# A hybrid scan and attention backbone on one core: the scan's decays in three wide operations, and the rotary tables made behind the scan

## The chip, the cores and the metric

The kernel runs on one core of a Trainium2 chip. The metric is the device time of one execution in microseconds, median of several runs. The core has TensorE (matmuls into PSUM), VectorE, ScalarE and GpSimd (elementwise work), and SyncE, whose queue SP issues every DMA of this kernel. Each engine works through a list of its own in order; semaphores join the lists. In the profile they are PE (PEld for its weight loads), DVE, ACT, POOL and SP.

## The reference

Two layers over 1024 latent and 256 context tokens, model width 1024. Each layer normalises and modulates its input, multiplies it by one input projection, and feeds three groups of heads: a bidirectional state space scan (8 heads of 64, 2 groups, state 128, chunks of 128 tokens), grouped-query attention and differential attention. Their outputs go through one output projection, a norm, a gate and the residual. The part that the change touches, cut:

```python
def ssd_scan(x, dt, a, bm, cm, init_state):
    xd = f(x * dt[..., None])
    a_cum = jnp.cumsum(f(dt * a), axis=2)
    lmat = segsum_exp(jnp.moveaxis(a_cum, -1, 2))
    y_diag = jnp.einsum('bcqhn,bcshn,bchqs,bcshp->bcqhp', cc, bc, lmat, xd)
    ...
    y_off = jnp.einsum('bcqhn,bchpn,bcqh->bcqhp', cc, states_in, jnp.exp(a_cum))
    return y_diag + y_off, final_state

def segsum_exp(cs):
    diff = cs[..., :, None] - cs[..., None, :]
    return jnp.exp(jnp.where(tril, diff, -jnp.inf))
```

So for each chunk and head there is a 128x128 matrix of decays exp(a_q - a_s) in each direction, weighted by the step size dt of the source token. And the queries and keys of the grouped-query heads are normalised and rotated by cosine and sine tables that depend on the position.

## The kernel before

All 10 token tiles (0 and 1 context, 2 to 9 latent) are kept as columns of 128 tokens. Per layer the work goes in stages:

- The transposed part of the input projection (x, B, C), a convolution over five taps and a SiLU (`conv_tile`). Beside it ScalarE and GpSimd split the output projection's weights (tile wos, `split_wout`), whose loads wof come over SP.
- The token-row part of the projection in five column chunks (`tok_chunk`): z, differential q and k, grouped q, k and v, differential v, gates. A chunk's weights are loaded (wf) and split into leading and trailing halves (wh, wl); then for each token tile 24 matmuls run into a bank prj, of which there are two. The bank goes off by ScalarE and VectorE: for z a tanh (th) on ScalarE and a product on VectorE; for q and k a copy raw (three buffers), rotation (`rope`), a split st, a transpose on TensorE (qps), a copy tt and stores.
- Beside the chunks z, differential q and k, and differential v runs the scan (`scan`), a generator that the loop over token tiles advances. Per chunk c it loads xb (x and B in token rows), ab (the running sums of both directions on all 128 partitions, 8 heads of 128 columns each, 1 MB, one buffer) and bct. D and W are the two halves of ab. VectorE subtracts each head's own sum (L775) and takes the minimum with the other direction's (L776), ScalarE takes the exponential of all of D (L778). Then for each head ScalarE multiplies the masked product gf of C and B by the forward step size into W (L781), VectorE adds the backward one (L782), and GpSimd multiplies W by D (L784). TensorE's 8 products of W with x (pd, L792) follow, and `y_off` (po, yt) and `state_step` (xs, stp, Sf, Sb) bring in the states. The next load of ab needs those products done.
- The chunk of grouped q, k and v runs when the scan is over, with the final norm of the scan's output (`finish`: yf, zt) between its token tiles. Its rotation needs the tables C and S (cosine and sine with the gains folded in), which before are made ahead of the scan: two loads (cosg, sing), four products on GpSimd (L933), four on VectorE (L934).
- The gates' chunk, then attention and the output projection.

The instructions are not in the order of the code: a scheduler, run when the program is built, goes by priorities and its own estimates of durations, and lays down one fixed list per engine. Pools are released tile by tile, and a later tile in the same memory waits for the readers of the earlier one. The lines that matter:

```python
D, W = ab[:, 0], ab[:, 1]
for h in range(8):
    V.tensor_scalar(D[:, h], D[:, h], acs[:, 0, c, h:h + 1], None, op0=ALU.subtract)
    V.scalar_tensor_tensor(D[:, h], W[:, h], acs[:, 1, c, h:h + 1], D[:, h],
                           op0=ALU.subtract, op1=ALU.min)
S_.activation(D, D, AF.Exp)
```

## Time and profile before

| what | value |
|---|---|
| time, median of 3 runs | 2101.39 us (2097.04 to 2106.61) |
| span of the profiled execution | 2095.2 us |
| TensorE busy | 1822.2 us (87%) |
| VectorE busy | 1565.1 us (75%) |
| ScalarE busy | 1041.9 us (50%) |
| GpSimd busy | 1162.7 us (55%) |
| mean granted TensorE clock | 0.935 |

The span is that of one profiled execution, from its first to its last instruction; the median is 6.2 us longer, and the runs lie from 1.8 to 11.4 us above the span. Busy time counts what an engine executes, and an operation that is held up while it runs counts as busy for all of it. The granted clock is the share of full speed that TensorE was given.

### The profile page before, as it was taken

To read this page: it belongs to the slowest core of one execution; us is meant where nothing else is said; L and a number is where in the kernel's file an instruction comes from. 1 tells how busy PE (TensorE), PEld (TensorE's weight loads), DVE (VectorE), ACT (ScalarE), POOL (GpSimd) and SP (SyncE) were. 2 spreads that over 40 slices of the span, in tenths; PEclk is the share of its full clock that TensorE was granted. 3 is DMA by queue.
4 is the path that set the end of the run, shared out by engine and by line. 5 is a ranking of instruction groups with operands and counts; after the bars stand their busy time and mean duration, and the time that the engine had idled before them with its cause. 6 is when DMAs were issued, how large, how long until landed. Compare 5 with 4: busy or idle time off the path is not lost.

```text
span 2095.2 us, 31014 instructions
## 1 busy us (share of the span) xinstructions
PE 1822.2 (87%) x9936; PEld 1475.8 (70%) x9936; DVE 1565.1 (75%) x4103; ACT 1041.9 (50%) x1955; POOL 1162.7 (55%) x1007
## 2 busy tenths in 40 slices
PE   5899999898979999888988797998798898989885
PEld 4587777777767668777765486877777776768773
DVE  5777567777759878799858477577687787888974
ACT  4444233334347766676634354233333676767651
POOL 4535355654227657668735335556543577877741
PEclk9899999899989999999989898998998999999997
DMA  9157557856795988586665148668656956457455
GB/s 289 44 197 235 174 178 205 265 176 203 213 267 167 283 257 261 165 248 201 216 218 186 33 151 283 207 188 247 218 157 208 278 172 180 140 157 212 145 183 184
DMA packets 360003, 418.61 MB, mean 200 GB/s; under 512 B 38752, under 2 KB 252832, under 8 KB 359840
## 3 DMA queue, kind: packets, MB, share of 16 engines
q1 hardware_dynamic: 359840, 416.64, 64.0%
q8 instruction: 78, 1.28, 0.2%
q14 instruction: 85, 0.70, 0.1%
HBM read 282.18 MB, written 134.38 MB: 199 GB/s over the span
## 4 chain that ended last, share of the span: by engine, by line
PE 38%; DVE 26%; DMA 16%; POOL 6%; issue 6%; ACT 4%; SPq 3%; DVEq 0%; POOLq 0%; ACTq 0%
DVE pt L1244 6%; PE sc L1242 4%; DMA ab<-acs 3%; PE tp L1373 3%; PE prj L962 3%; PE prj L961 3%; PE prj L963 3%; PE ops L343 2%; PE ops L344 2%; PE ops L345 2%; PE po L1416 2%; PE po L1415 2%; DMA op<-o 2%; DMA q<-dq 2%; DMA wof<-in_wout_dram 2%
## 5 line engine op out<-in xcount | busy, mean ns | idle before, releaser
L129 POOL TENSOR_TENSOR pl<-pf,ph 128x512 fp32r<-128x512 f32 x283 | 374.2, 1327 | 197.2 <-DVE ph L1395 80.4
L1244 DVE TENSOR_SCALAR_CACHE_REDUCE pt<-sc 128x512 f32<-128x512 f32 (+1 forms) x600 | 335.3, 587 | 71.6 <-PE sc L1242 62.8
L1257 ACT ACTIVATE pt<-pt,nm 128x1280 f32<-128x1280 f32 x192 | 262.4, 1366 | 132.1 <-DVE nm L1255 130.1
L961 PE MATMUL prj<-wh,u 128*128 128x512 f32 (+1 forms) x768 | 298.8, 391 | 27.1 <-DVE th L967 13.7
L962 PE MATMUL prj<-wl,u 128*128 128x512 f32 (+1 forms) x768 | 295.9, 386 | 8.0 <-POOL wl L129 5.3
L963 PE MATMUL prj<-wh,u 128*128 128x512 f32 (+1 forms) x768 | 293.9, 384 | 0.0
L1373 PE MATMUL tp<-ident,pt 128*128 128x128 f32 x1312 | 209.5, 283 | 4.9 <-ACT pf L1383 3.5
L1416 PE MATMUL po<-pl,vt 128*128 128x256 f32 x644 | 184.4, 308 | 18.6 <-POOL pl L129 14.9
L1415 PE MATMUL po<-ph,vt 128*128 128x256 f32 x644 | 187.7, 304 | 14.5 <-ACT ot L1420 6.3
L1383 ACT COPY pf<-tp 128x512 f32<-128x512 f32 x289 | 166.6, 580 | 66.3 <-PE tp L1373 30.9
L961 PEld LDWEIGHTS prj<-wh,u 128*128 128x128 f32 x768 | 153.1, 200 | 54.3 <-DVE th L967 15.6
L1373 PEld LDWEIGHTS tp<-ident,pt 128*128 128x128 f32 x1312 | 160.4, 145 | 29.5 <-ACT pf L1383 8.2
L962 PEld LDWEIGHTS prj<-wl,u 128*128 128x128 f32 x768 | 153.6, 200 | 33.5 <-POOL wl L129 6.6
L1242 PE MATMUL sc<-dk,q 128*128 128x512 f32 (+1 forms) x400 | 148.2, 416 | 31.2 <-DVE pt L1244 21.3
L963 PEld LDWEIGHTS prj<-wh,u 128*128 128x128 f32 x768 | 153.6, 200 | 23.2
L1416 PEld LDWEIGHTS po<-pl,vt 128*128 128x128 f32 x644 | 126.8, 197 | 39.4 <-POOL pl L129 27.4
L1415 PEld LDWEIGHTS po<-ph,vt 128*128 128x128 f32 x644 | 127.1, 197 | 29.5 <-ACT ot L1420 9.5
L607 DVE SCALAR_TENSOR_TENSOR cacc<-craw,hw,cacc 128x1284 f32<-128x1284 f32 (+1 forms) x64 | 118.5, 1853 | 33.4 <-ACT cacc L604 21.9
L582 PE MATMUL prj<-u,wTh 128*128 128x512 f32 x256 | 108.4, 423 | 23.4 <-DVE u L210 17.0
L343 PE MATMUL ops<-y,wo 128*128 128x512 f32 (+1 forms) x304 | 119.0, 391 | 7.4 <-DMA y<-y 6.8
L1296 POOL TENSOR_SCALAR pt<-pt,cc 128x256 f32<-128x256 f32 x64 | 103.1, 1612 | 38.1 <-DVE cc L1288 16.1
L1242 PE MATMUL sc<-gk,q 128*128 128x256 f32 (+1 forms) x400 | 111.7, 384 | 14.1 <-DVE pt L1244 11.8
(287 smaller groups left out, 4448.1 us busy)
## 6 DMA issues: line engine op xcount, KB each, us to landing
wo<-wo SPq DMA_DIRECT2D x80, 512.0 KB, 4.8
wm<-in_wmod_dram SPq DMA_DIRECT2D x48, 512.0 KB, 5.9
dk<-dk SPq DMA_DIRECT2D x16, 1280.0 KB, 7.9
ab<-acs SPq DMA_DIRECT2D x18, 1024.0 KB, 7.6
wo<-wos SPq DMA_DIRECT2D x32, 512.0 KB, 3.6
wf<-in_wtok_dram SPq DMA_DIRECT2D x64, 256.0 KB, 4.0
y<-y SPq DMA_DIRECT2D x30, 512.0 KB, 5.5
op<-o SPq DMA_DIRECT2D x48, 256.0 KB, 4.4
```

What stands on the lines that cost most here:

```text
L129: eng.tensor_tensor(out_, full, hi.bitcast(F32), op=ALU.subtract)
L343: TE.matmul(o, wa[:, k], y[:, :, 0], start=first, stop=False)
L961: TE.matmul(ps[:, c0:], uh, wh[k][:, c0:], start=k == 0, stop=False)
L962: TE.matmul(ps[:, c0:], uh, wl[k][:, c0:], start=False, stop=False)
L963: TE.matmul(ps[:, c0:], ul, wh[k][:, c0:], start=False, stop=k == KT - 1)
L1242: TE.matmul(ps[:, 0:b - a].rearrange("p (t c) -> p t c", c=P), q[:, jb.q0 + j], kt[:, a // P:b // P], start=x == 0, stop=x == len(qq) - 1)
L1244: V.tensor_scalar(ts[r][:, a:b], ps[:, 0:b - a], -1.0, None, op0=ALU.mult, op1=ALU.min, accum_out=mts[r][:, i:i + 1])
L1257: S_.activation(e, e, AF.Exp, bias=nm, scale=-1.0, accum_out=jb.s2[:, j, mp_:mp_ + 1])
L1373: TE.transpose(tp[:, j * P:(j + 1) * P], jb.pt[2 * hf + j % 2][:, cs(2 * s + j // 2)], ident)
L1383: S_.copy(pf[:, :w_], tp[:, :w_])
L1415: TE.matmul(o, vv, a[:, c], start=k == 0, stop=False)
L1416: TE.matmul(o, vv, b[:, c], start=False, stop=k == jb.nk - 1)
```

## The change

In the scan, GpSimd subtracts the sums of all heads from D in one operation of 128x1024, VectorE does it for W in one, and takes the minimum in one. The products with the forward step sizes go into a new tile rw (one buffer), those with the backward ones into W, all sixteen on ScalarE, and VectorE adds the two tiles in one operation. The rotary tables are made by a function `tables` that is called when the scan is over, in a pool `rot2` of its own that takes memory which the scan has left. Comments and docstrings are gone in the new file too, and below the scan its line numbers are 4 to 8 higher.

```diff
+        def over_q(tab_, dr, c):
+            return tab_[:, dr, c, :].unsqueeze(2).to_broadcast([P, 8, P])
...
                     D, W = ab[:, 0], ab[:, 1]
+                    G.tensor_tensor(D, D, over_q(acs, 0, c), op=ALU.subtract)
+                    V.tensor_tensor(W, W, over_q(acs, 1, c), op=ALU.subtract)
+                    V.tensor_tensor(D, W, D, op=ALU.min)
+                    S_.activation(D, D, AF.Exp)
+                    R = sp.tile([P, 8, P], F32, name="rw", tag="rw")
                     for h in range(8):
-                        V.tensor_scalar(D[:, h], D[:, h], acs[:, 0, c, h:h + 1], None, op0=ALU.subtract)
-                        V.scalar_tensor_tensor(D[:, h], W[:, h], acs[:, 1, c, h:h + 1], D[:, h],
-                                               op0=ALU.subtract, op1=ALU.min)
-                    S_.activation(D, D, AF.Exp)
+                        S_.activation(R[:, h], gf[:, 0, h // 4], AF.Copy, scale=dts[:, 0, c, h:h + 1])
                     yield
                     for h in range(8):
-                        S_.activation(W[:, h], gf[:, 0, h // 4], AF.Copy, scale=dts[:, 0, c, h:h + 1])
-                        V.scalar_tensor_tensor(W[:, h], gf[:, 1, h // 4], dts[:, 1, c, h:h + 1], W[:, h],
-                                               op0=ALU.mult, op1=ALU.add)
+                        S_.activation(W[:, h], gf[:, 1, h // 4], AF.Copy, scale=dts[:, 1, c, h:h + 1])
+                    V.tensor_tensor(W, W, R, op=ALU.add)
                     G.tensor_tensor(W, W, D, op=ALU.mult)
...
         with pool("rot") as rp, pool("tokc", 2) as ck:
-            cosg = ck.tile([P, 8, 32], F32, name="cosg", tag="st", bufs=2)
-            sing = ck.tile([P, 8, 32], F32, name="sing", tag="st", bufs=2)
-            SY.dma_start(cosg, ropeg[0])
-            SY.dma_start(sing, ropeg[1])
...
+            def tables(rp):
+                cosg = rp.tile([P, 8, 32], F32, name="cosg")
+                sing = rp.tile([P, 8, 32], F32, name="sing")
+                SY.dma_start(cosg, ropeg[0])
+                SY.dma_start(sing, ropeg[1])
...
-            with pool("trp2", 4, space=PSUM) as trp_, pool("fin", 2) as fp, pool("wsplit2", 2) as wo_:
+            with pool("trp2", 4, space=PSUM) as trp_, pool("fin", 2) as fp, pool("wsplit2", 2) as wo_, \
+                    pool("rot2") as rp2:
+                tables(rp2)
                 for t, _ in enumerate(tok_chunk(ck, 2, 0)):
```

The body of `tables` is the code that stood in the place of the dots: the gains gn, then the four products each.

What the scheduler makes of it, at three places. First VectorE's list at one chunk of the scan in layer 0; before:

```order
L721 TENSOR_TENSOR Sf<-stp,Sf 128x512
L775 TENSOR_SCALAR ab<-ab,acs 128x128 x6
L776 SCALAR_TENSOR_TENSOR ab<-ab,acs 128x128
L775 TENSOR_SCALAR ab<-ab,acs 128x128
...
L776 SCALAR_TENSOR_TENSOR ab<-ab,acs 128x128 x5
L782 SCALAR_TENSOR_TENSOR ab<-gf,dts,ab 128x128
L776 SCALAR_TENSOR_TENSOR ab<-ab,acs 128x128
L782 SCALAR_TENSOR_TENSOR ab<-gf,dts,ab 128x128 x4
L967 SCALAR_TENSOR_TENSOR th<-th,prj 128x512
```

and now, with GpSimd's list at a chunk some steps later behind it:

```order
L725 TENSOR_TENSOR Sf<-stp,Sf 128x512
L779 TENSOR_TENSOR ab<-ab,acs 128x1024
L973 SCALAR_TENSOR_TENSOR th<-th,prj 128x512
L780 TENSOR_TENSOR ab<-ab 128x1024
L788 TENSOR_TENSOR ab<-ab,rw 128x1024
```

```order
L778 TENSOR_TENSOR ab<-ab,acs 128x1024
L713 TENSOR_TENSOR xs<-xbb,coef 128x512
L895 TENSOR_TENSOR raw<-raw,t_2876 128x512
L723 TENSOR_TENSOR Sf<-Sf,etot 128x512
L129 TENSOR_TENSOR st<-raw,st 128x8x32
L789 TENSOR_TENSOR ab<-ab 128x1024
L723 TENSOR_TENSOR Sb<-Sb,etot 128x512
L895 TENSOR_TENSOR raw<-raw,t_2958 128x512
```

On VectorE the product th that frees a projection bank stands between the two wide operations, where it stood behind a row of small ones. On GpSimd the subtraction L778 stands ahead of the state inputs xs, a rotation sum raw and a split st; before, no operation of its list needed ab until L784.

Second, ScalarE's list where layer 1 passes from the convolution to the scan; before:

```order
L679 CAST wos<-wof 128x512
L625 COPY xt<-xtp 128x256
L625 COPY xt<-xtp 128x512 x2
L679 CAST wos<-wof 128x512 x2
L966 ACTIVATE th<-prj 128x512 x2
L679 CAST wos<-wof 128x512
L966 ACTIVATE th<-prj 128x512 x2
L778 ACTIVATE ab<-ab 128x1024
```

and now:

```order
L679 CAST wos<-wof 128x512
L972 ACTIVATE th<-prj 128x512 x2
L625 COPY xt<-xtp 128x256
L625 COPY xt<-xtp 128x512 x2
L679 CAST wos<-wof 128x512 x2
L972 ACTIVATE th<-prj 128x512
L679 CAST wos<-wof 128x512
L972 ACTIVATE th<-prj 128x512 x3
L781 ACTIVATE ab<-ab 128x1024
```

Two tanh moved ahead of the copies xt and two casts. In the scan's later chunks of the new list the eight products rw stand ahead of the exponential.

Third, VectorE's list behind the scan in layer 1, now:

```order
L907 TENSOR_TENSOR raw<-raw,nrr 128x384
L931 TENSOR_SCALAR gnqg<-pk_11893 128x64
L931 TENSOR_SCALAR gnkg<-pk_11893 128x64
L910 TENSOR_TENSOR raw<-raw,gnkg 128x128 x2
L940 SCALAR_TENSOR_TENSOR Skg<-sing,gnkg 128x8x32 x2
L940 SCALAR_TENSOR_TENSOR Sqg<-sing,gnqg 128x8x32 x2
L886 TENSOR_TENSOR t_15544<-raw,Sqg 128x4x32
```

The products with the sine table, which stood ahead of the scan's first chunk, stand right ahead of the first rotation (L886; L881 before). On SP the loads cosg and sing now follow the scan's last two stores of ys.

## Rows read from the trace of the kernel before

**Rows 1.** The page's first line.
```profile
span 2095.2 us, 31014 instructions
```

**Rows 2.** Busy time by stage: stretch, length, then PE, PEld, DVE, ACT, POOL, PEclk, DMA.
```profile
220.00:480.00 260.00, 235.47 (x1240) 199.53 (x1240) 184.58 (x438) 85.67 (x200) 140.97 (x115) 0.95 0.65 201
480.00:560.00 80.00, 68.58 (x306) 55.09 (x305) 66.21 (x255) 32.23 (x75) 34.27 (x38) 0.89 0.68 199
1310.00:1520.00 210.00, 186.33 (x1028) 161.98 (x1027) 142.30 (x314) 70.17 (x164) 117.74 (x97) 0.93 0.70 215
1520.00:1610.00 90.00, 81.32 (x383) 65.72 (x382) 80.12 (x303) 34.12 (x80) 40.67 (x48) 0.92 0.55 164
```

**Rows 3.** PE's waits in 220:480, then 1310:1520: us, times, longest.
```profile
PE po L727 <- DVE yt L729: 5.5, 4, 2.5
PE prj L961 <- DVE vs L129: 4.7, 1, 4.7
PE qps L843 <- DVE st L833: 4.6, 3, 1.9
...
PE gp L769 <- DVE gf L772: 1.6, 1, 1.6
...
PE qps L843 <- DVE st L833: 5.4, 6, 2.3
PE po L727 <- DVE yt L729: 4.8, 3, 3.4
...
PE prj L961 <- DVE vs L129: 2.8, 2, 2.2
...
PE prj L962 <- DVE wl L129: 1.5, 2, 1.1
```

**Rows 4.** The scan's lines: count, busy us, mean ns, idle before and its cause.
```profile
L776 DVE SCALAR_TENSOR_TENSOR ab<-ab,acs 128x128 f32<-128x128 f32 x144 | 55.4, 425 | 0.0
L782 DVE SCALAR_TENSOR_TENSOR ab<-gf,dts,ab 128x128 f32<-128x128 f32 x144 | 53.7, 422 | 0.9 <-ACT ab L781 0.8
L781 ACT ACTIVATE ab<-gf,dts 128x128 f32<-128x128 f32 x144 | 50.2, 393 | 77.0 <-DVE ab L776 70.9 <-DMA dq<-tt 5.2 <-DVE gf L771 0.3
L775 DVE TENSOR_SCALAR ab<-ab,acs 128x128 f32<-128x128 f32 x144 | 45.7, 373 | 46.8 <-DMA ab<-acs 34.4 <-DMA bct<-bc 7.4 <-DMA z<-th 5.1
L784 POOL TENSOR_TENSOR ab<-ab 128x1024 f32<-128x1024 f32 x18 | 44.8, 2486 | 38.2 <-DVE ab L782 35.5 <-issue 2.7
```

**Rows 5.** The same view: the nearest operations in kind and size.
```profile
L1292 DVE SCALAR_TENSOR_TENSOR pt<-pt,cc 128x1024 f32<-128x1024 f32 x64 | 92.2, 1441 | 0.7
...
L719 POOL TENSOR_TENSOR Sf<-Sf,etot 128x512 f32<-128x512 f32 x16 | 17.4, 1087 | 8.7 <-DVE Sf L717 4.6 <-PE po L727 4.1
```

**Rows 6.** Timelines of DVE and POOL in layer 0's scan: start us, us taken.
```profile
423.12 1.13 DVE L776 SCALAR_TENSOR_TENSOR ab<-ab,acs 128x128 f32<-128x128 f32 x1
...
425.16 0.34 DVE L776 SCALAR_TENSOR_TENSOR ab<-ab,acs 128x128 f32<-128x128 f32 x1
...
423.01 1.09 POOL L709 TENSOR_TENSOR xs<-xbb,coef 128x512 f32<-128x512 f32 x1 [2.75 <-DMA xbb<-xb]
```

**Rows 7.** PE's timeline ahead of layer 1's scan, the idle time in brackets.
```profile
1306.02 0.79 PE L961 MATMUL prj<-wh,u 128*128 128x512 f32 x1 [7.35 <-DVE th L967]
```

**Rows 8.** Last ys and first rotation, layers 0 and 1; tables' products; sing's landing.
```profile
472.71 0.32 SPq L818 DMA_DIRECT2D ys<-y  x1
473.14 0.29 DVE L881 TENSOR_TENSOR t<-raw,Sqg 128x128 f32<-128x128 f32 x1
...
1529.42 1.26 DVE L881 TENSOR_TENSOR t<-raw,Sqg 128x128 f32<-128x128 f32 x1
...
1535.52 0.32 SPq L818 DMA_DIRECT2D ys<-y  x1
...
222.38 1.84 DVE L934 SCALAR_TENSOR_TENSOR Sqg<-sing,gnqg 128x256 f32<-128x256 f32 x2
...
DMA to landing us min/median/max: 3.5/3.6/3.6
```

More of the change, by code (lines that the diff above doesn't have):

```diff
@@ L914, in block_kernel @@
             cosd, sind, nsind = rd[:, 0], rd[:, 1], rd[:, 2]
-            cosg = ck.tile([P, 8, 32], F32, name="cosg", tag="st", bufs=2)
-            sing = ck.tile([P, 8, 32], F32, name="sing", tag="st", bufs=2)
             SY.dma_start(rd, roped.rearrange("a p t c -> p a t c"))
-            SY.dma_start(cosg, ropeg[0])
-            SY.dma_start(sing, ropeg[1])
-            gain = {}
-            for n, sc in (("qg", 64 ** -0.5), ("kg", 1.0)):
-                gn = rp.tile([P, 64], F32, name=f"gn{n}")
-                V.tensor_scalar(gn, pc(n), sc, None, op0=ALU.mult)
-                gain[n] = gn
@@ L926, in block_kernel @@
-            tab = {}
-            for n in ("kg", "qg"):
-                c_ = rp.tile([P, 8, 2, 32], F32, name=f"C{n}")
-                s_ = rp.tile([P, 8, 2, 32], F32, name=f"S{n}")
-                for hf in range(2):
-                    ga = gain[n][:, hf * 32:hf * 32 + 32].unsqueeze(1).to_broadcast([P, 8, 32])
-                    gb = gain[n][:, 32 - hf * 32:64 - hf * 32].unsqueeze(1).to_broadcast([P, 8, 32])
-                    G.tensor_tensor(c_[:, :, hf, :], cosg, ga, op=ALU.mult)
-                    V.scalar_tensor_tensor(s_[:, :, hf, :], sing, -1.0 if hf == 0 else 1.0, gb,
-                                           op0=ALU.mult, op1=ALU.mult)
-                tab[n] = (c_, s_)
+            gain, tab = {}, {}
@@ new lines, in tables @@
+            def tables(rp):
[3 more added lines that the diff above has]
+                SY.dma_start(sing, ropeg[1])
+                for n, sc in (("qg", 64 ** -0.5), ("kg", 1.0)):
+                    gn = rp.tile([P, 64], F32, name=f"gn{n}")
+                    V.tensor_scalar(gn, pc(n), sc, None, op0=ALU.mult)
+                    gain[n] = gn
+                for n in ("kg", "qg"):
+                    c_ = rp.tile([P, 8, 2, 32], F32, name=f"C{n}")
+                    s_ = rp.tile([P, 8, 2, 32], F32, name=f"S{n}")
+                    for hf in range(2):
+                        ga = gain[n][:, hf * 32:hf * 32 + 32].unsqueeze(1).to_broadcast([P, 8, 32])
+                        gb = gain[n][:, 32 - hf * 32:64 - hf * 32].unsqueeze(1).to_broadcast([P, 8, 32])
+                        G.tensor_tensor(c_[:, :, hf, :], cosg, ga, op=ALU.mult)
+                        V.scalar_tensor_tensor(s_[:, :, hf, :], sing, -1.0 if hf == 0 else 1.0, gb,
+                                               op0=ALU.mult, op1=ALU.mult)
+                    tab[n] = (c_, s_)
```

## The prediction

> **What bounds the kernel now.** I read the page's first line, then the busy time by stage, then what TensorE waits for in the stages that the edit touches, then the lines of the scan. The profiled execution spans 2095.2 us [rows 1]; the median of the runs is 2101.39, 6.2 above it. The sum is made on the span, and its difference is put on the median. A difference of 0.5% (10.5 us) is about what a measurement can tell from none.
>
> The stage rows [rows 2] hold the scan of layer 0 (220 to 480 us), the chunk of attention columns behind it (480 to 560), and the same two of layer 1 (1310 to 1520, 1520 to 1610). In both scans TensorE is the busiest engine: 235.47 of 260 us and 186.33 of 210. [...] VectorE works 71% and 68% there, ScalarE a third, GpSimd 54% and 56%. TensorE runs its list in order, with the scan's matmuls strewn among the projection's, so a late VectorE result stops the projection too: the waits that name VectorE sum to 16.4 us in layer 0 (5.5 + 4.7 + 4.6 + 1.6) and 14.5 in layer 1 (5.4 + 4.8 + 2.8 + 1.5) [rows 3]. [...] Nothing outside these four stages is edited.
>
> **The change part by part.**
>
> *VectorE in the scan.* Eighteen chunks have 24 small operations each: 45.7 + 55.4 + 53.7 = 154.8 us in all [rows 4]. They become three of 128x1024. The trace has one like them in size and with both inputs in SBUF, 1441 ns in the mean [rows 5]: 3 x 18 x 1.441 = 77.8. VectorE gets 77 us back, 4.3 a chunk. The means of the small operations hold waiting: one that starts beside a GpSimd operation of 1.09 us takes 1.13 us and ends with it, where a free one takes 0.34 [rows 6].
>
> [...]
>
> How much of the 30.9 us of TensorE's waits goes? Bounds: nothing, since VectorE still waits for the load of ab (34.4 us in all [rows 4]) and now for GpSimd's part too; or all 30.9. VectorE's busy time in the two scans (326.9 us [rows 2]) falls by 77, 24%, and waits in a queue fall faster than its load; I take 40%: **-12.4 us**. [...]
>
> *ScalarE.* Eight more products a chunk, as dear as those there: +50.2 us [rows 4]. ScalarE has 174 and 140 us free in the two scans [rows 2]; the built order puts the eight new ones ahead of the exponential, while ab is still on its way, so they lie off the chain. *GpSimd.* One subtraction a chunk over 128x1024. Its floor is twice the broadcast product of 512, 2 x 1.087 = 2.17 us [rows 5], its ceiling the 2.49 of the full product [rows 4]; I take the floor, it has the same broadcast: +39.1 us, with 119 and 92 free [rows 2]. What these two do to TensorE is not shown by any row; bounds 0 and 24 (rival C); I take **+2**, near the present waits, of which only a few us name GpSimd.
>
> *The chain of a chunk* from ab's landing: before, 16 operations, the products behind them, GpSimd's 2.49. Now 2.17, then a minimum of 1.44, eight products, an addition of 1.44, GpSimd's 2.49. The first 16 cost 16 x 0.399 = 6.4 by their means [rows 4], now 3.6; the products pipelined with VectorE's additions, now they don't. Neither way is it clearly longer, so I cost its length at nothing. Its cover is the projection: in the built order some two and a half of its tiles, 24 matmuls each, lie between the pd matmuls of two chunks. If that cover goes, it is rival C.
>
> *The order at the scan's start in layer 1.* TensorE sits idle 7.35 us there because the two tanh that free its banks stand in ScalarE's list behind three copies xt and two casts wos that wait for loads [rows 7]. In the built order two tanh stand ahead of them. Bounds 0 and 7.35; the third tanh still stands behind the casts, so I take **-5**.
>
> *The tables.* Before, the two loads, four products on GpSimd and four on VectorE lie in front of the scan, where VectorE then waits for ab anyhow (46.8 us idle ahead of L775 in all [rows 4]); taking them from there saves nothing. Now the loads stand in SP's queue behind the scan's last two stores of ys, as their tiles reuse the scan's memory. Layer 0: last ys issued at 472.71, 0.3 for it, as much for cosg, 3.6 to sing's landing, 3.7 for the four products (two took 1.84) = 480.6, where the first rotation ran at 473.14: 7.5 us late. Layer 1: 1535.52 + 7.9 = 1543.4 against 1529.42: 14.0 late [rows 8]. All behind the tables in VectorE's list waits too: rotations, the gate products of the final norm, and by them GpSimd's rotation sums, the transposes on TensorE and SP's stores of q and k. VectorE has 13.8 and 9.9 us idle in these stages [rows 2], and TensorE runs ahead by two banks and three copies of the projection. So the floor is 14.0 - 9.9 = 4.1 and the ceiling 21.5. The idle time lies partly where VectorE waits for loads, not where it could catch up: I take the floor and a third of the other 17.4: **+9.9**.
>
> *Sum:* -12.4 - 7.1 + 2 - 5 + 9.9 = -12.6 us: span 2082.6, **2089 us** on the median.
>
> **The rivals.**
>
> *A: the waits on VectorE go altogether.* -30.9 - 17.8 + 2 - 5 + 9.9 = -41.8: **2060 us**. For it: nearly all these waits follow the small operations in the list. Against: VectorE's 34.4 us of waiting for ab stay.
>
> *B: the tables eat it.* All 21.5 us reach TensorE: -12.4 - 7.1 + 2 - 5 + 21.5 = -1, **2100 us**. For it: VectorE is at 89% in the stage of layer 1 [rows 2]. Against: TensorE's lead.
>
> *C: GpSimd becomes the one that is late; it ends slower.* Its list is in order, and the new subtraction waits for ab's landing as VectorE did, so behind it stand the inputs of the state matmuls, the rotation sums and the splits. Price: 34.4 us of such waiting and 39.1 of work, a third of it on TensorE = 24.5. Idle: -12.4 + 24.5 = +12.1, clock +7, then -5 + 9.9: +24, **2125 us**. [...] For it: the subtraction stands ahead of the state inputs in the built order. Against: GpSimd is idle for 45% of the scans.
>
> *D: the two engines shut each other out.* A row shows a VectorE operation ending with GpSimd's [rows 6]; if that holds for all of the new work, GpSimd's 39.1 us comes off the 77, half of the first two terms goes, and with -6.2 - 3.6 + 2 - 5 + 9.9 = -2.9 it is **2098 us**, the change not doing what it says. [...] Its size is open, as one long wait may take the place of many short.
>
> **How the numbers follow.** Forecast 0.45, A 0.15, B 0.16, C 0.13, D 0.11. The forecast's own range, 2076 to 2102, lies about two thirds under 2090.9 (faster by over 0.5%): 0.29 of its 0.45. With A that is 0.44 for faster; the other 0.16 with B and nearly all of D is 0.42 for within 0.5%; C and a rest of D 0.14 for slower. The range runs from 2062, which leaves out about half of A, to 2114, which leaves out most of C: some 0.19 outside.
>
> **What would show it.** In the scans: VectorE's three lines at some 78 us, TensorE's waits on VectorE near 18.5 us, those on GpSimd under 9, TensorE's idle time near 36 us at a granted clock of 0.95 to 0.97. At layer 1's start, a gap of 2 to 3 us in place of 7.35. Behind the scans, the first rotation some 7 and 14 us after where it was, and some 10 us more idle time on TensorE. The prediction is wrong if waits on VectorE stay at 30 us, if GpSimd's go over 9, or if the time comes from stages that are not edited, whose order is also laid anew.

## The result and the profile after

The changed kernel takes 2121.24 us (median of 4 runs, 2116.4 to 2123.38) against 2099.81 in the runs beside it: a ratio of 1.0093, interval 1.0074 to 1.0112. It is **slower by 0.93%**, where 2089 was forecast and 2114 was the upper end. The profiled execution grew by 23.6 us [rows 1]:

```profile
span 2118.8 us, 30796 instructions
...
PE 1823.4 (86%) x9936; PEld 1474.0 (70%) x9936; DVE 1529.4 (72%) x3725; ACT 1080.1 (51%) x2099; POOL 1211.5 (57%) x1025
```

TensorE is as busy as before (1822.2 us), VectorE is 35.7 us less busy. The place is found with the token-row part of the projection in each layer, from its first matmul to its last: the scan and the stage behind it. Busy time by stretch (stretch, length, PE, PEld, DVE, ACT, POOL, PEclk, DMA), before:

```profile
201.60:586.30 384.70, 346.59 (x1740) 288.75 (x1738) 268.99 (x722) 129.59 (x295) 176.54 (x154) 0.94 0.66 201
1283.80:1629.60 345.80, 304.75 (x1576) 257.63 (x1575) 241.58 (x644) 120.70 (x272) 176.23 (x156) 0.93 0.69 211
```

and after:

```profile
202.20:603.30 401.10, 348.81 (x1741) 288.75 (x1739) 241.40 (x512) 151.12 (x374) 209.21 (x164) 0.93 0.62 189
1297.90:1651.80 353.90, 304.99 (x1576) 256.54 (x1574) 225.00 (x476) 138.50 (x338) 203.49 (x164) 0.93 0.66 204
```

TensorE's idle time there, length less busy time, was 38.1 + 41.1 = 79.2 us and is 52.3 + 48.9 = 101.2. These 22.0 us are nearly the whole difference, and come though VectorE has 44 us less to do in the two stretches. Cut as in [rows 2], the two scans and the two stages behind them:

```profile
220.00:493.00 273.00, 232.23 (x1205) 195.72 (x1203) 153.53 (x215) 104.41 (x273) 170.40 (x121) 0.93 0.62 193
493.00:577.00 84.00, 72.68 (x328) 57.23 (x328) 71.33 (x274) 35.98 (x84) 36.56 (x42) 0.90 0.62 182
1324.00:1537.00 213.00, 177.95 (x988) 153.46 (x987) 119.53 (x139) 85.92 (x226) 141.34 (x101) 0.92 0.68 210
1537.00:1632.00 95.00, 83.90 (x391) 67.81 (x391) 84.00 (x307) 35.52 (x84) 45.58 (x52) 0.92 0.56 168
```

What TensorE waits for in the two scan stretches (us, times, longest), to be held against [rows 3]:

```profile
PE qps L848 <- DVE st L838: 6.2, 4, 2.2
PE prj L968 <- DVE wl L129: 5.8, 2, 3.7
PE po L731 <- DVE yt L733: 5.0, 2, 3.9
...
PE gp L773 <- DVE gf L776: 3.1, 3, 2.7
...
PE pd L797 <- POOL ab L789: 2.4, 2, 1.3
...
PE po L731 <- DVE yt L733: 8.3, 3, 5.1
PE qps L848 <- DVE st L838: 6.0, 3, 4.9
PE stp L719 <- POOL xs L713: 4.7, 3, 2.4
PE prj L968 <- DVE wl L129: 4.0, 4, 1.6
PE prj L967 <- DVE vs L129: 3.9, 3, 2.4
```

With the smaller rows, the waits that name VectorE are 25.6 + 27.0 = 52.6 us where they were, counted in the same way, 32.2: an engine with less work is waited for longer. Those that name GpSimd are 16.8 us where they were 5.3. Why, the scan's lines say (busy us, mean ns, idle before and its cause), against [rows 4]:

```profile
L778 POOL TENSOR_TENSOR ab<-ab,acs 128x1024 f32<-128x1024 f32 x18 | 51.0, 2834 | 54.4 <-DMA ab<-acs 54.4
...
L789 POOL TENSOR_TENSOR ab<-ab 128x1024 f32<-128x1024 f32 x18 | 43.6, 2424 | 27.7 <-DVE ab L788 27.7
...
L780 DVE TENSOR_TENSOR ab<-ab 128x1024 f32<-128x1024 f32 x18 | 34.1, 1893 | 18.6 <-POOL ab L778 18.6
L788 DVE TENSOR_TENSOR ab<-ab,rw 128x1024 f32<-128x1024 f32 x18 | 23.1, 1283 | 25.3 <-ACT ab L787 25.3
L779 DVE TENSOR_TENSOR ab<-ab,acs 128x1024 f32<-128x1024 f32 x18 | 22.1, 1225 | 68.1 <-DMA ab<-acs 68.1
```

VectorE's work fell as forecast, from 154.8 to 34.1 + 23.1 + 22.1 = 79.3 us. But its idle time ahead of this work rose from 47.7 (46.8 + 0.9) to 18.6 + 25.3 + 68.1 = 112.0. Work and waiting together: 202.5 before, 191.3 after. Of the 75.5 us saved, 64.3 became standing in the list, with all that is queued behind standing too. GpSimd's part went from 44.8 + 38.2 = 83.0 us to 176.7.

### The profile page after: what moved, and what is told of

Read it like the earlier page. It is cut to its first block, busy times and chain, and to the rows that moved or that the text cites. A ratio compares the mean times of both kernels' runs of the same rounds, so it can differ in the third digit from the quotient of the medians.

```text
span 2118.8 us, 30796 instructions
## 1 busy us (share of the span) xinstructions
PE 1823.4 (86%) x9936; PEld 1474.0 (70%) x9936; DVE 1529.4 (72%) x3725; ACT 1080.1 (51%) x2099; POOL 1211.5 (57%) x1025
## 4 chain that ended last, share of the span: by engine, by line
PE 28%; DVE 24%; DMA 12%; issue 5%; POOL 5%; ACT 4%; SPq 2%; DVEq 0%; POOLq 0%; ACTq 0%
DVE pt L1252 6%; PE sc L1250 3%; DMA ab<-acs 3%; PE tp L1381 3%; PE ops L343 2%; DMA q<-dq 2%; PE ops L344 2%; PE ops L345 2%; PE prj L967 2%; PE prj L968 2%; PE prj L969 2%; PE po L1424 2%; PE po L1423 2%; DVE pt L1300 1%; DMA y<-y 1%
## 5 line engine op out<-in xcount | busy, mean ns | idle before, releaser
L129 POOL TENSOR_TENSOR pl<-pf,ph 128x512 fp32r<-128x512 f32 x283 | 378.5, 1341 | 207.8 <-DVE ph L1403 99.3
L967 PE MATMUL prj<-wh,u 128*128 128x512 f32 (+1 forms) x768 | 298.4, 391 | 25.2 <-DVE th L973 8.5
L1424 PE MATMUL po<-pl,vt 128*128 128x256 f32 x644 | 182.6, 306 | 16.2 <-POOL pl L129 15.3
L969 PEld LDWEIGHTS prj<-wh,u 128*128 128x128 f32 x768 | 152.4, 199 | 23.1
L1250 PE MATMUL sc<-gk,q 128*128 128x256 f32 (+1 forms) x400 | 114.5, 389 | 16.2 <-DVE pt L1252 11.9
```

What stands on the lines that cost most here:

```text
L129: eng.tensor_tensor(out_, full, hi.bitcast(F32), op=ALU.subtract)
L967: TE.matmul(ps[:, c0:], uh, wh[k][:, c0:], start=k == 0, stop=False)
L969: TE.matmul(ps[:, c0:], ul, wh[k][:, c0:], start=False, stop=k == KT - 1)
L1250: TE.matmul(ps[:, 0:b - a].rearrange("p (t c) -> p t c", c=P), q[:, jb.q0 + j], kt[:, a // P:b // P], start=x == 0, stop=x == len(qq) - 1)
L1424: TE.matmul(o, vv, b[:, c], start=False, stop=k == jb.nk - 1)
```

## The experiments

In the table, time is against before by the runs of the same chip. "Stretch" is from the end of a chunk's last minimum to the start of GpSimd's product W times D, "period" from one issue of ab's load to the next, both means over the chunks (18 and 16 of them) worked out from the timelines. The idle time is TensorE's in the two token-row stretches, as above. Stretch, period and idle time come from one trace each.

| kernel | its difference | ratio [interval] | stretch | period | idle |
|---|---|---|---|---|---|
| before | | 1 | 4.1 | 25.3 | 79 |
| changed | | 1.0093 [1.0074, 1.0112] | 5.6 | 26.0 | 101 |
| e1_tables | tables late, scan as before | 1.0050 [1.0028, 1.0072] | 4.3 | 25.5 | 90 |
| e4_decays | e1 + wide decays | 1.0023 [1.0002, 1.0045] | 5.0 | 25.2 | 90 |
| e5_products | e1 + products on ScalarE | 0.9968 [0.9947, 0.9990] | 4.1 | 24.5 | 78 |
| e6_ab2 | e1 + two buffers ab | 1.0065 [1.0044, 1.0086] | 11.9 | 18.7 | 95 |
| e3_vsub | changed, both subtractions on VectorE | 1.0091 [1.0061, 1.0121] | 5.8 | 26.5 | 92 |
| e18_swap | changed, subtractions in the other order | 1.0071 [1.0049, 1.0094] | 5.5 | 26.0 | 101 |
| e8_own | changed, products in their own buffer | 1.0023 [1.0006, 1.0040] | 5.3 | 22.3 | 90 |
| e16_own_held | the same, last product in ab | 1.0046 [1.0028, 1.0065] | 3.2 | 24.4 | 80 |
| e17_exp_last | changed, exponential behind the products | 0.9995 [0.9978, 1.0012] | 4.8 | 24.6 | 79 |
| e9_prod_own | e5, products in their own buffer | 0.9996 [0.9977, 1.0014] | 4.0 | 21.5 | 89 |
| e10_prod_half | e5, half of the tables early | 1.0022 [1.0006, 1.0039] | 4.7 | 25.3 | 86 |
| e13_loads_early | e5, tables' loads and gains early | 0.9943 [0.9926, 0.9960] | 4.2 | 24.7 | 75 |
| e15_after_loads | changed, tables' loads and gains early | 1.0077 [1.0051, 1.0102] | 5.5 | 26.0 | 101 |
| e14_before_ct | before, ct in yp's buffer | 1.0103 [1.0082, 1.0124] | 4.3 | 25.7 | 94 |
| e11_prod_early | e14, products on ScalarE | 1.0004 [0.9987, 1.0021] | 5.4 | 25.5 | 77 |
| e12_scan_early | e11, wide decays | 1.0230 [1.0205, 1.0255] | 7.7 | 27.4 | 113 |
| e19_exp_loads | e17, tables' loads and gains early | 0.9970 [0.9952, 0.9988] | 4.8 | 24.8 | 82 |
| e20_small_exp_loads | e13, exponential behind the products | 0.9940 [0.9919, 0.9961] | 3.7 | 24.4 | 75 |

**The parts alone.** Three kernels with late tables: the scan as before; only the decays wide; only the products moved.

The last two, against the changed scan:

```diff
 # e4_decays: the products as before
-S_.activation(R[:, h], gf[:, 0, h // 4], AF.Copy, scale=dts[:, 0, c, h:h + 1])
-S_.activation(W[:, h], gf[:, 1, h // 4], AF.Copy, scale=dts[:, 1, c, h:h + 1])
-V.tensor_tensor(W, W, R, op=ALU.add)
+S_.activation(W[:, h], gf[:, 0, h // 4], AF.Copy, scale=dts[:, 0, c, h:h + 1])
+V.scalar_tensor_tensor(W[:, h], gf[:, 1, h // 4], dts[:, 1, c, h:h + 1], W[:, h],
+                       op0=ALU.mult, op1=ALU.add)
 # e5_products: the decays as before
-G.tensor_tensor(D, D, over_q(acs, 0, c), op=ALU.subtract)
-V.tensor_tensor(W, W, over_q(acs, 1, c), op=ALU.subtract)
-V.tensor_tensor(D, W, D, op=ALU.min)
+V.tensor_scalar(D[:, h], D[:, h], acs[:, 0, c, h:h + 1], None, op0=ALU.subtract)
+V.scalar_tensor_tensor(D[:, h], W[:, h], acs[:, 1, c, h:h + 1], D[:, h],
+                       op0=ALU.subtract, op1=ALU.min)
```

> The scan as before, only the rotary tables made late. Theory W (waiting in order): the loss is the scan's own, because the wide operations make VectorE and GpSimd stand for the landing of ab, for each other and for ScalarE; then this kernel is 0 to 8 us above before (2100 to 2108). Rival T (tables): most of the 21 us is the tables' move; then 15 to 21 us above before, and the idle time behind the scans is that of the changed kernel.

> The tables late and the decays by three wide operations, the products of the step sizes as before (ScalarE, then VectorE's small additions). Theory W: the wide decays carry most of the loss, 10 to 18 us above the kernel with the tables alone, VectorE and GpSimd each idle 50 us or more ahead of ab's operations. Rival P (products): the loss sits in the products, which no longer pipeline between ScalarE and VectorE; then within 5 us of the kernel with the tables alone.

> The tables late, the small decays as before, only the products moved to ScalarE with one wide addition. Theory W: within 6 us of the kernel with the tables alone. Rival P: 10 to 18 us above it, the multiplication behind the addition starting later in each chunk.

Measured: the tables +0.50%; the wide decays 0.27 of a per cent below that kernel; the moved products 0.82 below it. Neither of the last two costs anything alone. Theory W missed all three: the tables alone cost 9 us, a little over its range, and the decays lost nothing. Rival T missed too, and rival P, which had the decays right, missed the products, for which it expected a loss. If the parts added up, the changed kernel would stand 0.59% under before; it stands 0.93% over. The 1.5% between (32 us) came with the two together.

The tables' price is where it was looked for, behind the scans: from before to e1_tables TensorE's idle time behind the last pd of the two scans rose from 20.2 to 31.6 us, while that ahead of it stayed (59.0 and 58.3). In the changed kernel it is 26.8, and the larger part of the loss lies ahead of the last pd (74.4). Starts, durations and idle time of four rows of the changed kernel in layer 0 (SP's queue, then VectorE):

```profile
484.66 0.32 SPq L823 DMA_DIRECT2D ys<-y  x1
...
485.51 0.44 SPq L928 DMA_DIRECT2D sing<-in_ropeg_dram  x1
...
487.80 1.58 DVE L940 SCALAR_TENSOR_TENSOR Skg<-sing,gnkg 128x256 f32<-128x256 f32 x2 [1.91 <-DMA sing<-in_ropeg_dram]
...
491.02 1.08 DVE L886 TENSOR_TENSOR t<-raw,Sqg 128x128 f32<-128x128 f32 x1
```

The first rotation comes 6.4 us behind the last store of ys, where it came 0.4 behind [rows 8]: 6 us late; in layer 1 6.4 behind instead of 6.1 ahead, 12.5 late. In e1_tables the stall shows on TensorE, and GpSimd's rows give the reason:

```profile
473.76 1.58 POOL L938 TENSOR_TENSOR Ckg<-cosg,gnkg 128x256 f32<-128x256 f32 x2 [2.91 <-DMA cosg<-in_ropeg_dram]
475.30 1.76 POOL L938 TENSOR_TENSOR Cqg<-cosg,gnqg 128x256 f32<-128x256 f32 x2
477.03 2.18 POOL L129 TENSOR_TENSOR st<-raw,st 128x384 fp32r<-128x384 f32 x2
...
478.25 1.01 PE L847 MATMUL qps<-identr,st 128*128 128x128 f32 x6 [10.67 <-POOL st L129]
```

Those two st are of the context tiles, which need the gains but no table. They stand behind the tables' products and the wait for cosg in GpSimd's list, and their gains were made late as well, in memory of the scan.

**Rivals C and D of the prediction, and a control.**

```diff
-G.tensor_tensor(D, D, over_q(acs, 0, c), op=ALU.subtract)
+V.tensor_tensor(D, D, over_q(acs, 0, c), op=ALU.subtract)
```

> The changed kernel with GpSimd's subtraction given to VectorE. Rival C (GpSimd late) and rival D (the two engines shut each other out) of the prediction: 6 to 15 us below the changed kernel (2106 to 2115), VectorE's three operations shorter by the waits they hold. Theory X: the subtractions are 1.2 us each on VectorE, the minimum's end moves by under 1 us, and the time stays within 5 us of the changed kernel.

> A control: the changed kernel with the two wide subtractions written in the other order, so that VectorE's comes first. TensorE's list stays as it is, VectorE's and GpSimd's move by a few rows. No theory has a term for it: within 4 us of the changed kernel (2117 to 2125).

With no subtraction on GpSimd the time is the same, 1.0091, and TensorE's waits on GpSimd in the token-row stretches did not fall (28.0 us, 21.8 in the changed kernel). So the loss does not need that subtraction, and rival C falls as its cause. A gain from it that VectorE's added work cancels (101.9 us in the scan, where it was 79.3) isn't excluded. Rival D is not tested by it: VectorE's second subtraction, 1.23 us in the changed kernel, here takes 2.06 in the median of 18, and what lengthens it was not shown. The control differs less than was meant: by the two traces TensorE, VectorE, ScalarE and GpSimd run the same lists as in the changed kernel. So it shows what a repetition gives, 1.0071 after 1.0093 and 100.9 us of idle time after 101.2, and says nothing of an order laid anew. VectorE's rows with both subtractions:

```profile
L779 DVE TENSOR_TENSOR ab<-ab,acs 128x1024 f32<-128x1024 f32 x18 | 31.0, 1720 | 0.0
...
L788 DVE TENSOR_TENSOR ab<-ab,rw 128x1024 f32<-128x1024 f32 x18 | 22.9, 1270 | 32.7 <-ACT ab L787 32.7
L778 DVE TENSOR_TENSOR ab<-ab,acs 128x1024 f32<-128x1024 f32 x18 | 22.1, 1225 | 47.9 <-DMA ab<-acs 47.9
```

The wait ahead of the addition has grown, to 32.7 us for ScalarE's products. That pointed to the stretch behind the minimum.

**The stretch between minimum and product.** A chunk of the changed kernel (start, duration; VectorE, ScalarE, GpSimd):

```profile
252.70 1.23 DVE L779 TENSOR_TENSOR ab<-ab,acs 128x1024 f32<-128x1024 f32 x1 [4.38 <-DMA ab<-acs]
...
255.71 2.05 DVE L780 TENSOR_TENSOR ab<-ab 128x1024 f32<-128x1024 f32 x1 [1.20 <-POOL ab L778]
...
261.23 1.23 DVE L788 TENSOR_TENSOR ab<-ab,rw 128x1024 f32<-128x1024 f32 x1 [3.47 <-ACT ab L787]
...
257.80 1.06 ACT L781 ACTIVATE ab<-ab 128x1024 f32<-128x1024 f32 x1 [6.00 <-DVE ab L780]
258.76 2.44 ACT L787 ACTIVATE ab<-gf,dts 128x128 f32<-128x128 f32 x8
...
252.76 2.92 POOL L778 TENSOR_TENSOR ab<-ab,acs 128x1024 f32<-128x1024 f32 x1 [6.73 <-DMA ab<-acs]
...
262.54 2.40 POOL L789 TENSOR_TENSOR ab<-ab 128x1024 f32<-128x1024 f32 x1 [5.86 <-DVE ab L788]
```

The second eight products are written over W, so they wait for the minimum, which still reads W; then the exponential stands ahead of them on ScalarE, and VectorE stands still for 3.47 us until they are done. Before, each head's product could start with that head's minimum, and the additions ran beside the other heads' products. A chunk of the kernel before (ScalarE, then VectorE):

```profile
400.13 0.40 ACT L781 ACTIVATE ab<-gf,dts 128x128 f32<-128x128 f32 x1 [5.14 <-DVE ab L776]
...
401.82 0.98 ACT L781 ACTIVATE ab<-gf,dts 128x128 f32<-128x128 f32 x3
...
403.75 1.06 ACT L778 ACTIVATE ab<-ab 128x1024 f32<-128x1024 f32 x1
...
403.11 0.34 DVE L782 SCALAR_TENSOR_TENSOR ab<-gf,dts,ab 128x128 f32<-128x128 f32 x1
403.37 0.34 DVE L776 SCALAR_TENSOR_TENSOR ab<-ab,acs 128x128 f32<-128x128 f32 x1
```

There the exponential did not stand ahead: in 16 of 18 chunks seven of the eight products come before it on ScalarE, and so they do in e5_products, where the decays are small. In the changed kernel none does, in any chunk. In e4_decays none does either, but there the additions are small and follow the products one by one, and VectorE's idle time ahead of them is 8.1 us and not 25.3. That is how two parts that cost nothing alone can cost together. Three kernels shorten the stretch, in different ways. The buffer of their own (e8_own; e16_own_held writes GpSimd's result to W again, and ab stays taken until pd):

```diff
-S_.activation(W[:, h], gf[:, 1, h // 4], AF.Copy, scale=dts[:, 1, c, h:h + 1])
-V.tensor_tensor(W, W, R, op=ALU.add)
-G.tensor_tensor(W, W, D, op=ALU.mult)
+S_.activation(Q[:, h], gf[:, 1, h // 4], AF.Copy, scale=dts[:, 1, c, h:h + 1])
+V.tensor_tensor(Q, Q, R, op=ALU.add)
+G.tensor_tensor(Q, Q, D, op=ALU.mult)
```

and e17_exp_last, one line moved:

```diff
-S_.activation(D, D, AF.Exp)
 ...
 for h in range(8):
     S_.activation(W[:, h], gf[:, 1, h // 4], AF.Copy, scale=dts[:, 1, c, h:h + 1])
+S_.activation(D, D, AF.Exp)
 V.tensor_tensor(W, W, R, op=ALU.add)
```

> The changed kernel with the second half of the products in a buffer of its own, so that products and addition need neither ab nor the minimum, and ab comes free with the multiplication and not with pd. Theory X (chain): in the changed kernel these products are written over W, so they wait for the minimum and then for the exponential ahead of them on ScalarE, and the multiplication starts 5.57 us after the minimum's end where it was 4.12; with buffers of their own it starts under 2.5 us after, and the kernel is 8 to 18 us below the changed one (2103 to 2113). Rival S (the wide subtractions and the minimum hold VectorE and GpSimd): within 5 us of the changed kernel (2116 to 2126).

> The changed kernel with the products in a buffer of their own, but GpSimd's last product written to W in ab, so that ab stays taken until pd as in the changed kernel. Theory X1 (the products' standing behind the minimum and the exponential is the loss): as fast as with the own buffer, 2103 to 2113. Rival X2 (what gained was ab's coming free earlier): within 4 us of the changed kernel (2117 to 2125).

> The changed kernel with the exponential behind the second half of the products in ScalarE's list, not ahead of it: VectorE's addition can start 1.05 us sooner in each chunk, and runs beside the exponential. X1: the multiplication starts 0.8 to 1.1 us sooner after the minimum's end (4.5 to 4.8 instead of 5.57), VectorE's 25.3 us of idle time ahead of the addition fall by 10 or more, and the time by 3 to 9 us (2112 to 2118). If the stretch between minimum and multiplication does not matter: within 3 us of the changed kernel.

e17_exp_last is the clearest: the time fell by 0.98 of a per cent, 20 us, more than expected (3 to 9), to that of before, with every operation of the change still there. Its chunk, in the same view:

```profile
256.89 2.05 DVE L780 TENSOR_TENSOR ab<-ab 128x1024 f32<-128x1024 f32 x1 [1.20 <-POOL ab L778]
...
261.46 1.23 DVE L788 TENSOR_TENSOR ab<-ab,rw 128x1024 f32<-128x1024 f32 x1 [2.52 <-ACT ab L786]
...
258.98 2.45 ACT L786 ACTIVATE ab<-gf,dts 128x128 f32<-128x128 f32 x8 [6.02 <-DVE ab L780]
261.33 1.05 ACT L787 ACTIVATE ab<-ab 128x1024 f32<-128x1024 f32 x1
```

and two of its scan's lines:

```profile
L788 DVE TENSOR_TENSOR ab<-ab,rw 128x1024 f32<-128x1024 f32 x18 | 23.6, 1310 | 17.5 <-ACT ab L786 17.3
L779 DVE TENSOR_TENSOR ab<-ab,acs 128x1024 f32<-128x1024 f32 x18 | 23.2, 1290 | 52.8 <-DMA ab<-acs 52.7
```

The exponential now runs beside VectorE's addition. The stretch is 0.8 us shorter, the period 1.4; VectorE's wait ahead of the addition fell by 7.8 us (10 was expected), that for ab by 15.3, and TensorE's idle time by 22. With its own buffer but ab held, the stretch is 2.4 us shorter and 0.47 of a per cent came back, between the two ranges expected. TensorE's idle time in the token-row stretches did come back, to 80 us; but what lies between the two stretches, which nothing edits, took 708 us where the changed kernel took 694. With ab free early as well, 0.70 came back, in theory X's range of time (2109.06 us); but there the stretch shrank by 0.2 us and not to under 2.5, because GpSimd came later to the product, behind other work (it sat idle for 8.5 us ahead of all 18 products), and the gain went with the period.

An edit also makes the scheduler lay the lists anew. Of the 3315 matmuls of the two token-row stretches 944 stand elsewhere in TensorE's list in e17_exp_last than in the changed kernel, 1280 in e16_own_held, 1005 in e19_exp_loads (below), 867 in e3_vsub. So e17_exp_last alone doesn't part the chain from the order. The kernels together do, as far as one trace of each can: the three with a stretch of at most 4.8 us have 79, 80 and 82 us of idle time, in three different orders; the three with one of 5.5 or more (changed, e15_after_loads, e3_vsub) have 101, 101 and 92, though e3_vsub's order is about as far from the changed kernel's as e17_exp_last's. The other kernels with wide decays fit in: e4_decays and e8_own have 90 us at 5.0 and 5.3, e12_scan_early 113 at 7.7. So the loss goes with the place of the second products in the chunk's chain; how many of the 20 us are the order's is open, and so is how much of e8_own's gain is ab's and how much the chain's. Among the kernels with small decays idle time does not follow the stretch: 75 to 94 us at 3.7 to 5.4 (e6_ab2 apart).

**Two buffers for ab, and the small-decay kernel with its own buffer.**

> The tables late, the scan as before, and ab in two buffers (8 KB more, from the room that the late tables leave), so that its load of 7.7 us runs beside the chunk before. Theory W: the chunks form a loop through the single ab, and VectorE's waiting for it (46.8 us ahead of the first small operation) stops what is queued behind; with it gone 15 to 30 us below the kernel with the tables alone. Rival L (the projection's list sets the pace, the loop does not bind): within 5 us of the kernel with the tables alone, though VectorE's idle time ahead of ab falls below 15 us.

> Small decays as before, products on ScalarE with the wide addition, all in buffers of their own. Theory X: the products there already end 0.8 us behind the exponential, so little is left on the chain: within 5 us of the same kernel without the buffer (2092 to 2102). Rival S': whatever frees ab sooner gains, 5 to 10 us below it.

The edits are `bufs=2` on ab's tile in e1_tables, and Q, as above, in e5_products. The loop through ab is real: with two buffers a chunk takes 18.7 us instead of 25.5, and the last pd of layer 0 ends at 424.5 us, 38 earlier than in e1_tables. Yet the time is 0.15 of a per cent above e1_tables, 4 us, as rival L has it: the projection beside the scan ended no sooner (593.1 us against 587.6). VectorE's idle time ahead of ab fell only to 26.9 us, where both readings wanted less, and its small operations took longer: L775 of before takes 379 ns in the mean in e1_tables, 556 here. e9_prod_own missed both readings: 6 us above e5_products, with the shorter period (21.5 against 24.5). In these two kernels, whose decays are small, a shorter period gained nothing; what sets the pace there was not looked into.

**The tables' price.** The edit of e13_loads_early and e15_after_loads (e10_prod_half made the keys' tables early as well, and loaded cosg again for the rest):

```diff
+cosg = rp.tile([P, 8, 32], F32, name="cosg")
+sing = rp.tile([P, 8, 32], F32, name="sing")
+SY.dma_start(cosg, ropeg[0])
+SY.dma_start(sing, ropeg[1])
+for n, sc in (("qg", 64 ** -0.5), ("kg", 1.0)):
+    gn = rp.tile([P, 64], F32, name=f"gn{n}")
+    V.tensor_scalar(gn, pc(n), sc, None, op0=ALU.mult)
+    gain[n] = gn
 def tables(rp2):
...
+    table(rp2, "kg", cosg, sing)
+    table(rp2, "qg", cosg, sing)
```

> Small decays as before, products on ScalarE; half of the rotary tables (the keys') and one of the two source tables made ahead of the scan again, the other half late. If the late tables cost 9 us by the work and the loads that stand ahead of the rotations, half of it comes back: 3 to 8 us below the same kernel with all tables late (2089 to 2094). If they cost by the first wait alone, or not by the tables but by the order laid anew: within 3 us of it.

> Small decays, products on ScalarE with the wide addition (the fastest so far, 2097), all eight products of the tables late, but their two source loads and the two gains ahead of the scan. In the kernel with the tables alone TensorE's longest wait behind the scan of layer 0, 10.7 us, goes back to the context tiles' gain products, that wait for gains whose buffer lies in the scan's memory, and VectorE waits 2.2 us for sing. If that is the tables' price: 4 to 9 us below (2088 to 2093), idle time behind the scans 8 us less (24.0 to 16). If the price is the products themselves or the order laid anew: within 3 us.

> The changed kernel with the two source loads of the tables and the two gains ahead of the scan, the products of the tables late as they are. The same edit took 5 us off the kernel with the small decays. If the tables' price is these loads and gains here too: 3 to 9 us below the changed kernel (2112 to 2118). If the scan's loss hides it (VectorE and TensorE are late anyhow when the tables come): within 3 us of it.

e13_loads_early came to 2091.80 us, 0.25 of a per cent below e5_products and 0.57% below before, in its range, though the idle time behind the scans fell by 5.6 us and not by 8. In the changed kernel the same edit gave 0.16, as the second reading has it; with the stretch short (e19_exp_loads, below) it gave 0.25, which the two intervals don't part from nothing. e10_prod_half missed both readings, at 2108.25 us: its idle time behind layer 0's scan fell from 15.5 to 7.8 us, but that in the scan rose from 25.6 to 34.1.

**The products and the scan with early tables, and their control.** To make room, ct took yp's buffer, and the products went by four heads with 2 KB for R:

```diff
-ct = sp.tile([P, 2, P], F32, name="ct", tag="ct")
+ct = sp.tile([P, 2, P], F32, name="ct", tag="yp")
 # e11_prod_early, e12_scan_early
+for e in (0, 4):
+    R = sp.tile([P, 4, P], F32, name="rw", tag="rw")
+    for h in range(4):
+        S_.activation(R[:, h], gf[:, 0, e // 4], AF.Copy, scale=dts[:, 0, c, e + h:e + h + 1])
+        S_.activation(W[:, e + h], gf[:, 1, e // 4], AF.Copy, scale=dts[:, 1, c, e + h:e + h + 1])
+    V.tensor_tensor(W[:, e:e + 4], W[:, e:e + 4], R, op=ALU.add)
```

> Kernel before with only the products moved: both on ScalarE, four heads at a time with an addition of 128x512 each (2 KB instead of 4), ct in the buffer of yp for room, the tables ahead of the scan as before. If the products' gain (13.7 us, from the two kernels with late tables) and the tables' price (9 us) are independent: 2085 to 2093. If the order that is laid anew moves as much as the edits do: 2094 to 2108.

> The same with the three wide decays as well: the changed scan nearly whole (products by fours), the tables as before. Theory X+T: the changed scan costs 8 to 12 us and the tables 9, so 2106 to 2113 (by fours the addition starts sooner, so rather the lower end). Rival T2 (all of the loss is in the tables, by way of what they do to the scan's order): 2095 to 2104.

> A control for the two kernels above: kernel before, with nothing changed but ct in yp's buffer. No theory has a term for it: within 4 us of before. If an edit with no work in it moves the time by over 6 us, then differences of that size between the kernels above can come from the order that is laid anew, and are not put down to their edits.

The control is the miss that matters: this line alone costs 1.03%. It adds a wait (us, times, longest),

```profile
PE po L727 <- DMA ct<-bc: 3.7, 2, 2.8
```

in layer 1, but its list is also laid anew: 1744 of TensorE's 9936 matmuls stand elsewhere, idle time in the token-row stretches rose by 14.5 us, and what lies between them, attention of layer 0 and the transposed projection of layer 1, which nothing edits, took 14.5 us longer (711.6 against 697.1). So e11 and e12 say little in absolute terms: e11_prod_early came to 2104.06 us, in the range of an order that moves as much as the edits, and e12_scan_early to 2151.86, some 40 us above both of its ranges. Against the control the products gain again (-0.99 of a per cent) and the wide decays on top of them lose again (+2.3): the same signs as with late tables.

**A version that beats both.**

> The changed kernel with the exponential behind the products and with the tables' source loads and gains ahead of the scan. If the loads and gains give what they gave with small decays: 4 to 9 us below the kernel with the exponential moved alone (2094 to 2099). If the price of the tables is hidden here: within 3 us of it (2100 to 2106).

> Small decays, products on ScalarE, loads and gains ahead of the scan (2092), with the exponential behind the products. There the products end only 0.8 us behind the exponential, since the first of them run between the decays; so the addition gains under 1 us a chunk, and the multiplication now waits for the exponential: within 4 us of 2092. If it is over 5 us below, the exponential's place counts here too.

e19_exp_loads, the whole change with the exponential behind the products and the tables' loads and gains early, is 0.30% faster than before (2094.80 us). The small decays with ScalarE's products, e13_loads_early and e20_small_exp_loads, are 0.57 and 0.60% faster (2091.80, 2090.08), and between those two nothing can be told. All three came out where one of their readings had them. In e19_exp_loads, though, the idle time in the token-row stretches is 82 us where e17_exp_last has 79, so the place of that gain isn't shown. And all these gains are smaller than the 1.03% that the control moved: they are measured for these builds, and not shown to be their edits' alone. Nothing here shows that the wide decays pay.

## Why the prediction was wrong

**The step that failed** is the chain of a chunk: "Neither way is it clearly longer, so I cost its length at nothing", with two and a half of the projection's tiles as cover. The first eight products do lie off the chain, as said. It put the other eight behind the minimum and the addition behind them, but left out the exponential that stands ahead of them on ScalarE, and set the lost pipelining against shorter decays. These were to fall from 6.4 to 3.6 us; from the first operation to the last minimum's end a chunk took 5.9 before and 5.4 after, since GpSimd's subtraction takes 2.83 and the minimum 1.89. So the decays gave 0.5 us, and the stretch behind them took 1.5. In the kernel that took back 0.8 of it the time fell by 20 us. The cover protects TensorE only from a late pd (2.4 + 1.0 us of waits, 0.8 before). It does not protect it from what stands behind the chain's operations in VectorE's list: TensorE's waits for wl rose from 1.5 to 9.8 us, for gf from 2.0 to 6.4, for yt from 10.3 to 13.3.

**The terms, one by one.** VectorE's work: forecast 77.8 us, measured 79.3, right. Waits on VectorE: forecast 18.5, measured 52.6; in place of -12.4 came +20.4. The ground for it was that waits fall faster than load, the author's estimate; here the engine is waited for while it stands, 64.3 us longer than before. No run shows the clock's -7.1 in the sum, nor what the rivals' sums have for the clock (17.8, 7 and 3.6): the granted clock was 0.95 and 0.93 in the scans before and 0.93 and 0.92 after. GpSimd's new work: forecast 39.1, ceiling 2.49 each; measured 51.0, 2.83 each, above the ceiling; the one subtraction that ran without VectorE's beside it took 1.89, under the floor. For what the new work of ScalarE and GpSimd does to TensorE the sum had +2; the waits on GpSimd alone rose by 11.5. The start of layer 1's scan: the 7.35 us gap [rows 7] is gone; no such row is left, which is a little more than the -5. The tables: forecast +9.9, alone they cost 0.50%, 10.5 us; the rotations 7.5 and 14.0 us late, measured 6 and 12.5. Right in place, and near in size, though one build doesn't show a size to better than the control's 1%.

One figure on the way doesn't come out: 57% of the range 2076 to 2102 lies under 2090.9, not two thirds. It does not enter the forecast's sum.

**The rivals.** A fell, and B too: the tables cost 10.5 us and not 21.5. C named almost this time (2125) and its condition seemed met: waits on GpSimd in the scans, under 9 us in the forecast, are 16.8 by the same rows as above. But without GpSimd's subtraction the time is the same, so, as far as that shows, the number was near by luck. D exists in kind (the minimum took 1.21 us free and 2.05 beside GpSimd's work, as below), but not in size: VectorE's work fell by 75.5 us, close to the 77 forecast, and not by half of that. What none of them held is that parts which cost nothing alone cost 1.5% together.

The range was too narrow in one way that the control shows: an edit without work moved this kernel by 1%, by a wait of a few us and by lists laid anew. No term stood for that. Single differences of about 0.5% between these kernels, e10_prod_half's above all, stay open for that reason. Two kernels that stayed put are no test of it: e18_swap runs the changed kernel's lists, and in e15_after_loads only 170 of the 3315 token-row matmuls stand elsewhere. What speaks for the chain is that three kernels with a shorter stretch, in three orders, have the idle time of before in the edited stages, and that e3_vsub, in another order with the stretch as long, has the changed kernel's time.

## What to carry to other kernels

Before many small operations are made one wide one, write down what each small one let start early, on every engine of the chain; here the wide addition waited for the last of ScalarE's products, 25.3 us in all where the small ones waited 0.9. Count idle time ahead of an engine's work with its busy time: here 64.3 of the 75.5 us saved on VectorE returned as standing in its ordered list, and TensorE's waits on it in the scans rose from 32.2 to 52.6 us. Where products share an engine with a long operation that only the next but one step needs, try that operation last; and look where the scheduler put it before, since there the small operations may have kept it out of the way.

## What the runs showed of the hardware

A wide operation on VectorE with both inputs in SBUF took 1.21 us free and 2.05 beside GpSimd's work (the minimum, fastest and median of 18); GpSimd's subtraction took 1.89 us at its fastest, the one time that VectorE's did not run beside it, and 2.87 at its median (ns, least, median, most):

```profile
L780 DVE TENSOR_TENSOR ab<-ab x18: 1212/2050/2316, 230.8 to 1531.0; 128x1024 f32<-128x1024 f32 x18
...
L778 POOL TENSOR_TENSOR ab<-ab,acs x18: 1892/2872/2972, 227.9 to 1528.1; 128x1024 f32<-128x1024 f32 x18
```

Either takes longer beside the other's work, by about 0.8 and 1.0 us, and in these rows it is the one that starts later. VectorE's subtraction began 0.01 to 0.14 us ahead of GpSimd's in 17 chunks and took 1.22 to 1.23 us in each, while GpSimd's took 2.85 to 2.97. The minimum took 1.75 to 2.32 us in the 15 chunks where a GpSimd operation was under way at its start, and 1.21 to 1.23 in the 3 where none was. By what mechanism no run shows. The price here is 18 x 1.21 = 21.8 against the 34.1 us of the minimum, some 12 us of VectorE's time in 18 chunks. Whether these reach the end no run shows; in e17_exp_last, as fast as before, the minimum still takes 36.1 us.
